# Neighbourhood scores with zero-padded queries, bias and maximum in one instruction, and new planned lengths

## The chip, the cores and the metric

The kernel runs on one core of one Trainium2 chip. The metric is device time in microseconds (us). The figure for the kernel before is the median of three runs. A profile of one further execution supplies every duration below; its span runs from the first to the last instruction of the program, and the execution's own time lies a little above it.

The engines are TensorE (PE in the profile; PEld is its weight loads), VectorE (DVE), ScalarE (ACT), GpSimd (POOL) and SyncE (SP, which here only issues DMAs). TensorE reads SBUF and writes PSUM. Each engine works through its own list of instructions in order and waits on semaphores for the others.

## The reference

Two layers of a diffusion backbone. 256 latent tokens (a grid of 4 rows of 64 columns) and 128 context tokens pass through each layer with the same weights. A layer normalises and modulates its input, projects it once (`w_in`), and splits the columns among three head groups: latent attention (6 heads, "mla"), neighbourhood attention (6 heads of 64, "na"), and differential attention (4 heads, two softmax maps each, "diff"). The outputs are concatenated, projected by `w_out`, added to the residual through a gate, and followed by a gated feed-forward network. The part that the change touches is the neighbourhood attention:

```python
s_win = jnp.einsum('bhrqd,bhrjkd->bhrqjk', qg, kg).astype(jnp.float32) * scale + bias[None].astype(jnp.float32)
s_win = jnp.where(in_win[:, None, :], s_win, NEG)
s_ctx = jnp.einsum('bhrqd,bhcd->bhrqc', qg, k_ctx).astype(jnp.float32) * scale
...
p = jax.nn.softmax(jnp.concatenate([s_win.reshape(b, h, rows, GRID_W, n_win), s_ctx], axis=-1), axis=-1).astype(v.dtype)
```

A latent query thus sees 128 cached context keys without a bias and 256 latent keys with one: the learned bias of the relative position inside a window of 16 columns, and -1e30 outside it. The 128 context queries see the 128 context keys alone. The head size is 64.

## The kernel before

All 384 tokens lie in three tiles of 128 (two latent, `t` = 0 and 1, and one context, `t` = 2). Weights arrive by DMA in `raw` tiles, ACT rounds them to a high part (`wh`, `split_hi`, L254), DVE subtracts to get the low part (`wl`, L260), and each product of the large projections is three matmuls, L321 to L323 (`mm3`).

A layer's front and attention run under a planner. `add` makes a `Task` with an engine, a planned length, the tasks that it follows, the rooms that it takes (`z`, `s` and `t` are PSUM banks; `tok`, `brief`, `e`, `pT`, `pd`, `bias` are SBUF buffers) and a priority. `Plan.order` (L115) simulates all engines with these planned lengths and with `HOPS`, the time from one engine's end to another's start. Whenever an engine is free it takes the ready task of the lowest priority number whose rooms are free. It also models the clock of PE in windows of `WINDOW` = 3.413 us, and doubles PE's planned lengths when a window was little used. The starting times that come out fix the order of the instructions on all five engines; on the chip, an instruction waits in that order, whatever is ready behind it. Planned lengths therefore change no work, only its order.

The dense part of the plan is `g1`, the input projection in six groups of columns (`CHUNKS`): units of six matmuls with the priority `DENSE`, so that they fill PE's time between steps of attention. After them the first three blocks of the output projection (`OUT_EARLY`) play the same part. They write tiles that reuse the space of the dense part's inputs (`o_late`), so most of them can only follow when the dense part is done. Behind the plan, the rest of the output projection and the feed-forward network follow in the order of the program's text, with an order found by the framework's own scheduler.

The path of a neighbourhood head:

- `done_n(j)` takes columns of `g1` for the pair of heads 2j and 2j+1. Per token tile it copies them (L1184), squares (L1199), reduces (L1220), takes the root on POOL (L541, L542), scales (L1223), transposes queries and keys with PE (`turn`, L1209), and writes them to SBUF: `queries` on ACT (L1212) with the gain `naq`, `keys` on DVE (L1215). A pair's two heads lie in rows 0 to 63 and 64 to 127 of the tiles `nu[0]` (queries) and `nu[1]` (keys).
- `near(j)` calls `pair`, which calls `soft` five times: for each of the two heads and the two latent tiles a score of 128 queries against 384 keys, and then both heads' context scores of 128 by 128. `score` (L1037) is one call in float32, which appears as two matmul records, over the 64 rows of its head. `maxima` adds the bias in PSUM (L1100) and finds the maximum (L1045). `exps` (L1056) makes the exponentials and sums on ACT, `norm` the reciprocal (L1061) and the scaling (L1066) on DVE, `turn` transposes the map (L1004), and `evac` copies it out (L1106). When all is there, `out` multiplies by the values (L1139, L1142).
- The bias of a head is a tile of 128 by 6 x 64 floats, loaded from a table that the host builds (`_bias_index`), with two buffers (L1092).
- The latent heads use the same `soft` and `pair` with 96 rows, the differential heads `soft` with 128 rows.

The order of the attention steps is `mla(0)`, `diff(0)`, `mla(1)`, `mla(2)`, and then by `ORDER` `diff(1)`, `diff(2)`, `near(0)`, `diff(3)`, `near(1)`, `near(2)`.

Of the kernel before, what the change touches and what calls it, by code (L numbers as in the profile page):

```python
# [17 lines left out]
P = 128  # L18
# [39 lines left out]
HOPS = {('pe', 'act'): 0.2, ('pe', 'dve'): 0.16, ('act', 'pe'): 0.22, ('dve', 'pe'): 0.27, ('pool', 'dve'): 0.06, ('act', 'dve'): 0.15, ('dve', 'act'): 0.15}  # L58
# [124 lines left out]
def trunk(ctx: ExitStack, tc, xT_d, cv_d, crow_d, pcol_d, prow_d, cache_d, dfk_d, rope_d, bias_d, ident_d,  # L183
# [378 lines left out]
    def parameters(l, staged=None):  # L562
# [14 lines left out]
        naq, lam, nlam, subg = (par.tile([P, 1], F32, tag=t, name=nm(t)) for t in ("naq", "lam", "nlam", "subg"))  # L577
# [35 lines left out]
    for l in range(DEPTH):  # L613
# [177 lines left out]
        def g1(ci, done, kbs=(0, 2, 4, 6), kind="z"):  # L791
# [3 lines left out]
            for kb in kbs:  # L795
# [3 lines left out]
                for t in range(3):  # L799
# [7 lines left out]
                    u = add(PE, 6 * (n / 2400 + 0.003), unit, after=[lo, last[t], hready[kb], hready[kb + 1]],  # L807
# [95 lines left out]
        def up_q(t, pr):  # L903
# [37 lines left out]
            p = add(POOL, 1.6, lambda: rsqrt(x["rs"], x["ms"], 96 * EPS), after=red, prio=pr)  # L941
# [5 lines left out]
        def up_kv(i, pr):  # L947
# [34 lines left out]
            p = add(POOL, 1.6, lambda: rsqrt(x["rs"], x["ms"], mskr[:, i:i + 1]), after=red, prio=pr)  # L982
# [38 lines left out]
        def soft(maps, after, spread, bias=None, joint=None, keep=None):  # L1021
# [18 lines left out]
            def maxima():  # L1040
                if bias:
                    bias(x["b"][0][0])
                x["mx"], i = small(n), 0
                for ps, c in x["b"]:
                    nc.vector.tensor_reduce(x["mx"][:, i:i + c], ps[:, :c, :], axis=AX.X, op=ALU.max, negate=True)  # L1045
                    i += c

            def exps():
                x["su"], x["e"] = small(n), []
                for ps, c in x["b"]:  # L1050
                    for j in range(c):
                        i = len(x["e"])
                        if nk == NT or i == 0:
                            t = e_tile()
                        x["e"].append(t if nk == NT else t[:, i * nk:(i + 1) * nk])
                        nc.scalar.activation(x["e"][i], ps[:, j, :], AF.Exp, bias=x["mx"][:, i:i + 1],  # L1056
                                             accum_out=x["su"][:, i:i + 1])
# [14 lines left out]
            a = add(PE, COST_S * w / NT * (0.25 if joint else 1), score, after=after, take=("s",) * banks, prio=pr + PRS)  # L1072
            b = add(DVE, 0.08 * banks + 1.05e-3 * w + (0.34 if bias else 0), maxima, after=[a], prio=pr + PRM)
# [11 lines left out]
        def pair(kt, qk, v, h0, biased, after, vals, late=None):  # L1085
# [3 lines left out]
            for i in range(2) if biased else ():  # L1089
                def fetch(i=i):  # L1090
                    p["bias", i] = wk.tile([P, 6, 64], F32, tag="bias", name=nm("bias"))
                    nc.sync.dma_start(p["bias", i], bias_d[l, :, h0 + i])  # L1092
                ld[i] = add(DMA, 0.3, fetch, take=("bias",), prio=seq[0])
                in_line("bias", ld[i])
            vs, scored, rooms = [], [], []
            for i in range(2):
                for t in range(2):
                    def bias(ps, i=i, t=t):
                        u0 = 2 - 2 * t
                        nc.vector.tensor_tensor(ps[:, 0, P:NT], ps[:, 0, P:NT],  # L1100
                                                p["bias", i][:, u0:u0 + 4, :].rearrange("p u c -> p (u c)"), op=ALU.add)
# [15 lines left out]
                    else:  # L1117
# [51 lines left out]
        nu, na_ready, na_room = [], [[] for _ in range(3)], []  # L1169
        vn, vn_ready = [], [[] for _ in range(3)]  # L1170

        def na_units():
            nu.extend(units(3, P))
            dma.dma_start(nu[1][:, :, 0:P], cache_d[l, :, CA_NAK:CA_NAK + 384].rearrange("p (a b) -> p a b", a=3))

        def done_n(j):
            hd = slice(2 * j, 2 * j + 2)

            def done(t, z, unit, room):
# [31 lines left out]
                def queries():  # L1211
                    nc.scalar.activation(nu[0][:, j, t * P:(t + 1) * P], x["pt"][:, 0], AF.Copy, scale=naq)  # L1212
# [16 lines left out]
                na_ready[j].append(add(ACT, 0.26, queries, after=[f], frees=[f], prio=pr))  # L1229
# [6 lines left out]
        def done_d(p):  # L1236
            hd = slice(2 * p, 2 * p + 2)

            def done(t, z, unit, room):
# [45 lines left out]
                d = add(POOL, 1.9, lambda: rsqrt(x["rs"], x["ms"], EPS), after=[c], prio=pr)  # L1285
                e = add(DVE, 0.33, lambda: nc.vector.tensor_tensor(heads(x["n"], 8), heads(x["n"], 8), bc3(x["rs"], 32), op=ALU.mult),
                        after=[d], prio=pr)
                df_ready[p][t] = add(DVE, 1.25 if t < 2 else 0.34, rotate, after=[e], frees=[a], prio=pr)
# [4 lines left out]
        def df_unit(h, after, pr):  # L1293
# [19 lines left out]
            for t in range(3):  # L1313
# [29 lines left out]
                d = add(POOL, 0.86, parts_lo, after=[c], prio=pr)  # L1343
                e = add(PE, 0.37, stack, after=[d], take=("t",), frees=[c], prio=pr)
# [7 lines left out]
        def diff_step(h, t, st, after, late=()):  # L1352
# [30 lines left out]
            o = add(PE, 0.6 if t < 2 else 0.16, out, after=[v] + vd_ready[h // 2], take=("t",), frees=[x["room"]], prio=pr + PRO)  # L1383
# [3 lines left out]
        def diff_tail(h, st, late, pr):  # L1387
# [23 lines left out]
            c = add(POOL, 1.0, lambda: rsqrt(st["rs"], st["ms"], EPS), after=[b], prio=pr)  # L1411
# [41 lines left out]
        def near(j):  # L1453
            if not dense:
                dense.extend(t for t in plan.tasks if t.dense)
            sl = [slice(64 * i, 64 * i + 64) for i in range(2)]
            pair(3 + j, lambda: [[u[s, j, :] for s in sl] for u in nu], lambda: vn[min(j, 1)][:, :, slice(0, 2) if j < 2 else slice(2, 4)], 2 * j, True, na_ready[j], vn_ready[j],
                 "row" if j < 2 else "direct")

# [22 lines left out]
        for i, (ms, kb, r) in enumerate(blocks):  # L1482
# [5 lines left out]
            prev = add(PE, 0.93, lambda ms=ms, kb=kb: ms.mm(kb), after=[ld, prev, fin], frees=[ld] if ld else [], prio=DENSE / 2)  # L1488
# [144 lines left out]
def _bias_index():  # L1633

    p = np.arange(P)
# [8 lines left out]
    return np.where(inw[:, None, :], idx, 15 * 31)  # L1644
# [89 lines left out]
```

## Time and profile before

| | |
|---|---|
| median of three runs | 1035.77 us (1035.76 to 1036.49) |
| the profiled execution | 1036.13 us |
| its span | 1034.4 us |
| mean granted TensorE clock | 0.986 |
| PE busy | 1012.3 us, 6074 matmul records |
| DVE, ACT, POOL busy | 719.5, 509.1, 172.7 us |
| DMA | 162.25 MB, mean 157 GB/s |

The span has four kinds of stages. The first hundred us load and project; attention of layer 0 ends near 214 us; the output projection and feed-forward network of layer 0 run to about 530 us; layer 1 has its attention from about 575 to 723 us and its feed-forward network to the end. Busy time of PE is taken from matmul records whose ends are modelled, so the starts of successive records are the better measure of what a piece costs. A clock figure of 1.00 in the windows view means full clock and 0.50 half.

### The profile page before, as it was taken

The page shows a single profiled execution, that of the slowest core. Times are in us where ns is not written, and L with a number is a line of the kernel's source. Part 1 is how long each engine was busy: PE and PEld are TensorE (multiplying, and loading weights), DVE is VectorE, ACT ScalarE, POOL GpSimd, SP SyncE. Part 2 cuts the span into 40 slices and gives each one's busy share as a digit, 9 for nine tenths or more (in the row PEclk, how much of TensorE's full clock was granted, in tenths as well). Part 3 has the DMA queues.
Part 4 walks back from the last instruction along what each step waited for, and adds up shares of the span by engine and source line. Part 5 has one row for each costly group of instructions (what it writes and reads, how often), then busy time and mean ns, then how long its engine had stood idle before and what let it go on. Part 6 is the DMA issues. An engine that isn't in the chain of part 4 may idle for free.

```text
span 1034.4 us, 16528 instructions
## 1 busy us (share of the span) xinstructions
PE 1012.3 (98%) x6074; PEld 933.0 (90%) x6074; DVE 719.5 (70%) x1599; ACT 509.1 (49%) x1180; POOL 172.7 (17%) x263
## 2 busy tenths in 40 slices
PE   8999999989999999999999999989999999999998
PEld 7877779679999999999978878867999999999998
DVE  5677787955999999963455887766869755554332
ACT  3466778745433333343326668766653334333221
POOL 2266223201001001100024533230010000000000
PEclk9999999989999999999999999969999999999999
DMA  9865444125575757684463232410376434343441
GB/s 356 331 202 190 161 153 138 58 82 202 165 243 185 233 177 232 206 273 131 123 226 101 81 125 71 154 54 9 123 249 199 125 120 137 108 123 111 139 137 42
DMA packets 129681, 162.25 MB, mean 157 GB/s; under 512 B 5056, under 2 KB 111680, under 8 KB 127296
## 3 DMA queue, kind: packets, MB, share of 16 engines
q1 hardware_dynamic: 121184, 132.76, 40.3%
q0 software_dynamic: 6832, 27.77, 7.7%
q8 instruction: 48, 0.79, 0.3%
q10 hardware_dynamic: 1584, 0.66, 0.2%
q14 instruction: 33, 0.27, 0.1%
HBM read 158.12 MB, written 3.05 MB: 156 GB/s over the span
## 4 chain that ended last, share of the span: by engine, by line
PE 76%; DVE 2%; ACT 1%; POOL 1%; issue 1%; ACTq 0%; DVEq 0%; POOLq 0%
PE z L321 11%; PE z L323 11%; PE z L322 11%; PE t L322 6%; PE t L321 6%; PE t L323 6%; PE s L322 5%; PE s L323 5%; PE s L321 5%; PE s L1037 2%; PE t L1004 2%; PE t L1139 1%; POOL small L542 1%; PE t L1376 1%; PE z L1037 1%
## 5 line engine op out<-in xcount | busy, mean ns | idle before, releaser
L254 ACT ACTIVATE wh<-raw 128x1024 fp32r<-128x1024 f32 (+2 forms) x216 | 201.5, 934 | 366.0 <-PE z L322 138.8
L260 DVE TENSOR_TENSOR wl<-raw,wh 128x1024 fp32r<-128x1024 f32 (+2 forms) x216 | 230.7, 1070 | 111.6 <-ACT wh L254 111.2
L321 PE MATMUL z<-fh,wh 128*128 128x386 f32 x304 | 103.2, 339 | 0.0
L322 PE MATMUL z<-fl,wh 128*128 128x386 f32 x304 | 103.0, 339 | 0.0
L323 PE MATMUL z<-fh,wl 128*128 128x386 f32 x304 | 102.6, 338 | 0.0
L444 DVE CUSTOM_DVE_ANT_0 sums<-wt,sums,pcol 128x1024 f32<-128x1024 f32 x80 | 102.2, 1278 | 0.3 <-DVE small L1578 0.3
L321 PE MATMUL z<-wh,hh 128*128 128x384 f32 (+1 forms) x264 | 99.9, 379 | 1.1 <-ACT hh L514 0.5
L323 PE MATMUL z<-wh,hl 128*128 128x384 f32 (+1 forms) x264 | 90.3, 342 | 0.5 <-DVE hl L522 0.5
L322 PE MATMUL z<-wl,hh 128*128 128x384 f32 (+1 forms) x264 | 89.8, 340 | 0.0
L542 POOL TENSOR_TENSOR small<-small,mhalf 128x4 f32<-128x4 f32 (+4 forms) x58 | 73.2, 1262 | 4.8
L321 PE MATMUL s<-fh,wh 128*128 128x386 f32 x200 | 68.2, 341 | 0.0
L321 PE MATMUL t<-fh,wh 128*128 128x386 f32 x200 | 68.1, 340 | 0.0
L322 PE MATMUL t<-fl,wh 128*128 128x386 f32 x200 | 67.8, 339 | 0.0
L322 PE MATMUL s<-fl,wh 128*128 128x386 f32 x200 | 67.8, 339 | 0.0
L323 PE MATMUL t<-fh,wl 128*128 128x386 f32 x200 | 67.5, 338 | 0.0
L323 PE MATMUL s<-fh,wl 128*128 128x386 f32 x200 | 67.5, 338 | 0.0
L438 POOL DMA_DIRECT2D wt<-in_w_modT x40 | 21.5, 539 | 273.7 <-DVE mod L444 190.8
L321 PEld LDWEIGHTS z<-wh,hh 128*128 128x128 f32 x264 | 49.8, 189 | 9.2 <-issue 4.2
L322 PEld LDWEIGHTS z<-fl,wh 128*128 128x128 f32 x304 | 57.5, 189 | 0.0
L323 PEld LDWEIGHTS z<-fh,wl 128*128 128x128 f32 x304 | 57.3, 188 | 0.0
L321 PEld LDWEIGHTS z<-fh,wh 128*128 128x128 f32 x304 | 57.2, 188 | 0.0
L1056 ACT ACTIVATE e<-s,small 128x384 f32<-128x384 f32 (+1 forms) x102 | 51.0, 506 | 12.2 <-DVE small L1045 11.2
(316 smaller groups left out, 2422.8 us busy)
## 6 DMA issues: line engine op xcount, KB each, us to landing
raw<-in_w_gate SPq DMA_DIRECT2D x22, 1024.0 KB, 6.0
raw<-in_w_up SPq DMA_DIRECT2D x22, 1024.0 KB, 5.4
raw<-in_w_down SPq DMA_DIRECT2D x32, 704.0 KB, 4.8
wt<-in_w_modT POOLq DMA_DIRECT2D x40, 512.0 KB, 4.3
raw<-in_w_mod SPq DMA_DIRECT2D x16, 1024.0 KB, 5.0
raw<-in_w_in SPq DMA_DIRECT2D x40, 384.0 KB, 3.9
raw<-in_w_out SPq DMA_DIRECT2D x8, 1024.0 KB, 5.5
qu<-in_w_mod SPq DMA_DIRECT2D x8, 512.0 KB, 7.4
```

Of the source, the lines that this page charges most:

```text
L254: nc.scalar.activation(hi, src, AF.Copy)
L260: nc.vector.tensor_tensor(lo, src, hi.bitcast(F32), op=ALU.subtract)
L321: nc.tensor.matmul(out, sh, mh, start=first, stop=False)
L322: nc.tensor.matmul(out, sh, ml, start=False, stop=False)
L323: nc.tensor.matmul(out, sl, mh, start=False, stop=last)
L438: nc.gpsimd.dma_start(self.w[:, self.loaded % 3], w_modT[l, c * P:(c + 1) * P])
L444: nc.vector.tensor_tensor_reduce(self.junk, self.w[:, self.n % 3], self.s[:, v], 1.0, pcol[l][:, PC_BMOD + c:PC_BMOD + c + 1], ALU.mult, A ...
L542: nc.gpsimd.tensor_tensor(out, t[:, :n], mhalf[:, :n], op=ALU.pow)
L1004: nc.tensor.transpose(pt[:, b, :], x, ident)
L1037: nc.tensor.matmul(ps[:, i, :], q, k, start=True, stop=True)
L1056: nc.scalar.activation(x["e"][i], ps[:, j, :], AF.Exp, bias=x["mx"][:, i:i + 1], accum_out=x["su"][:, i:i + 1])
L1139: nc.tensor.matmul(po[64 * i:64 * i + 64, 0:NL], vv[:, b, v0 + i, :], p["pT"][i][:, b, :], start=(b == 0), stop=(b == 2), tile_position=(0 ...
```

## The change

Five edits.

1. **Padded queries.** `queries` now writes each head into a tile of its own, 128 rows high. The gain `naq` becomes two columns, each with zeros in the other head's 64 rows, so that one ACT instruction per head writes its queries and zeros. That is two instructions of 128 by 128 in place of one. Four such tiles exist (the three columns of `nu[0]` and a new tile `qn`); heads take them in turn, so pair 2 reuses those of pair 0. The keys stay as they are, both heads above each other, and a score contracts over all 128 rows.
2. **A new order constraint.** For that reuse, the transposes of pair 2 (`na_last`) follow all scores of `near(0)`, its context scores included.
3. **Context scores in one bank.** Both heads' context scores now go to one PSUM bank, and one reduction finds both maxima.
4. **Bias and maximum in one pass.** `tensor_tensor_reduce` adds the bias to all 384 keys, multiplies by -1, writes back to PSUM and gives the minimum, which is the negated maximum that `exps` needs. The exponential then uses scale -1. The bias tile grows to 128 by 5 x 128 floats, with a block of zeros for the context keys; a query tile takes blocks 0, 2, 4 or 0, 1, 2.
5. **Planned lengths.** `HOPS` and the planned lengths of some dozen tasks change; nothing that they stand for is changed.

```diff
-HOPS = {('pe', 'act'): 0.2, ('pe', 'dve'): 0.16, ('act', 'pe'): 0.22, ('dve', 'pe'): 0.27, ('pool', 'dve'): 0.06, ('act', 'dve'): 0.15, ('dve', 'act'): 0.15}
+HOPS = {('pe', 'act'): 0.22, ('pe', 'dve'): 0.22, ('act', 'pe'): 0.22, ('dve', 'pe'): 0.27, ('pool', 'dve'): 0.18, ('dve', 'pool'): 0.18, ('act', 'dve'): 0.15, ('dve', 'act'): 0.13}
...
+            nc.vector.memset(naq, 0.0)
+            for i in range(2):
+                h = slice(64 * i, 64 * i + 64)
+                nc.vector.tensor_scalar(naq[h, i:i + 1], pc[h, PC_NAQ:PC_NAQ + 1], 0.125, None, op0=ALU.mult)
...
-                    u = add(PE, 6 * (n / 2400 + 0.003), unit, after=[lo, last[t], hready[kb], hready[kb + 1]],
+                    u = add(PE, 6 * (n / 2400 + 0.0135), unit, after=[lo, last[t], hready[kb], hready[kb + 1]],
...
-            p = add(POOL, 1.6, lambda: rsqrt(x["rs"], x["ms"], 96 * EPS), after=red, prio=pr)
+            p = add(POOL, 2.1, lambda: rsqrt(x["rs"], x["ms"], 96 * EPS), after=red, prio=pr)
...
             def maxima():
+                x["mx"], i = small(n), 0
                 if bias:
-                    bias(x["b"][0][0])
-                x["mx"], i = small(n), 0
+                    s = x["b"][0][0][:, 0, :]
+                    s = s.rearrange("p (b k) -> p b k", k=P)
+                    nc.vector.tensor_tensor_reduce(s, s, bias(), -1.0, 3e38, ALU.add, ALU.min, x["mx"])
+                    return
...
-                                             accum_out=x["su"][:, i:i + 1])
+                                             scale=-1.0 if bias else 1.0, accum_out=x["su"][:, i:i + 1])
...
-            a = add(PE, COST_S * w / NT * (0.25 if joint else 1), score, after=after, take=("s",) * banks, prio=pr + PRS)
-            b = add(DVE, 0.08 * banks + 1.05e-3 * w + (0.34 if bias else 0), maxima, after=[a], prio=pr + PRM)
+            a = add(PE, (0.22 if joint else COST_S) * w / NT, score, after=after, take=("s",) * banks, prio=pr + PRS)
+            b = add(DVE, 0.08 * banks + 1.05e-3 * w + (0.06 if bias else 0), maxima, after=[a], prio=pr + PRM)
...
-                    p["bias", i] = wk.tile([P, 6, 64], F32, tag="bias", name=nm("bias"))
+                    p["bias", i] = wk.tile([P, 5, P], F32, tag="bias", name=nm("bias"))
...
-            x, a, e, pr = soft(lambda: [(qk()[0][i][:, NL:NT], qk()[1][i][:, NT:512], i == 0 or biased) for i in range(2)], after,
-                               (P, 2, 2 if biased else 1), keep="pd")
+            x, a, e, pr = soft(lambda: [(qk()[0][i][:, NL:NT], qk()[1][i][:, NT:512], i == 0) for i in range(2)], after,
+                               (P, 2, 1), keep="pd")
...
+            qn = ws.tile([P, NT], F32, name=nm("qn"))
+            nu[0] = [nu[0][:, i, :] for i in range(3)] + [qn]
...
-                    nc.scalar.activation(nu[0][:, j, t * P:(t + 1) * P], x["pt"][:, 0], AF.Copy, scale=naq)
+                    for i in range(2):
+                        nc.scalar.activation(nu[0][(2 * j + i) % 4][:, t * P:(t + 1) * P], x["pt"][:, 0], AF.Copy, scale=naq[:, i:i + 1])
...
+                if j == 2:
+                    na_last.append(f)
-                na_ready[j].append(add(ACT, 0.26, queries, after=[f], frees=[f], prio=pr))
+                na_ready[j].append(add(ACT, 0.53, queries, after=[f], frees=[f], prio=pr))
...
-            pair(3 + j, lambda: [[u[s, j, :] for s in sl] for u in nu], ...
+            scored, _ = pair(3 + j, lambda: [[nu[0][(2 * j + i) % 4] for i in range(2)], [nu[1][:, j, :]] * 2], ...
+            for t in na_last if j == 0 else ():
+                for a in scored:
+                    a.then.append(t)
+                    t.need += 1
```

Further planned lengths, old to new: the roots on POOL 1.6 to 2.1, 1.9 to 2.2 and 1.0 to 1.18; the rotation of differential heads 1.25 to 1.35 and 0.34 to 0.42; their low parts on POOL 0.86 to 0.98; their stacking on PE 0.37 to 0.47; their product with the values 0.6 to 0.67 and 0.16 to 0.23; a block of modulation matmuls 0.93 to 1.0.

More of the change, by code (lines that the diff above doesn't have):

```diff
@@ L1090, in fetch @@
                 def fetch(i=i):
-                    p["bias", i] = wk.tile([P, 6, 64], F32, tag="bias", name=nm("bias"))
+                    p["bias", i] = wk.tile([P, 5, P], F32, tag="bias", name=nm("bias"))
                     nc.sync.dma_start(p["bias", i], bias_d[l, :, h0 + i])
-                ld[i] = add(DMA, 0.3, fetch, take=("bias",), prio=seq[0])
+                ld[i] = add(DMA, 0.6, fetch, take=("bias",), prio=seq[0])
                 in_line("bias", ld[i])
@@ L1166, in mla_pair @@
             return pair(j, lambda: [[mlu[h // 3][w][:, h % 3, :] for h in hs] for w in range(2)], lambda: vm, 2 * j, False, after, vals)
-        nu, na_ready, na_room = [], [[] for _ in range(3)], []
+        nu, na_ready, na_room, na_last = [], [[] for _ in range(3)], [], []
         vn, vn_ready = [], [[] for _ in range(3)]
@@ L1342, in df_unit @@
                 c = add(ACT, 0.56, parts_hi, after=[a, df_ready[h // 2][t]], take=("tok",), prio=pr)
-                d = add(POOL, 0.86, parts_lo, after=[c], prio=pr)
-                e = add(PE, 0.37, stack, after=[d], take=("t",), frees=[c], prio=pr)
+                d = add(POOL, 0.98, parts_lo, after=[c], prio=pr)
+                e = add(PE, 0.47, stack, after=[d], take=("t",), frees=[c], prio=pr)
                 out.append(add(ACT, 0.27, queries, after=[e], frees=[e], prio=pr))
@@ L1382, in diff_step @@
             v = add(ACT, 0.38 if t < 2 else 0.2, evac, after=[e], frees=[e], prio=pr + PRT)
-            o = add(PE, 0.6 if t < 2 else 0.16, out, after=[v] + vd_ready[h // 2], take=("t",), frees=[x["room"]], prio=pr + PRO)
+            o = add(PE, 0.67 if t < 2 else 0.23, out, after=[v] + vd_ready[h // 2], take=("t",), frees=[x["room"]], prio=pr + PRO)
             st["kept"] = st.get("kept", []) + [add(ACT, 0.2, keep, after=[o], frees=[o], prio=pr + PRO)]
@@ L1410, in diff_tail @@
                     after=[a], frees=[a], prio=pr)
[L1411 removed]
+            c = add(POOL, 1.18, lambda: rsqrt(st["rs"], st["ms"], EPS), after=[b], prio=pr)
             d = add(DVE, 0.28, scaled, after=[c] + ([st["mate"]] if h % 2 else []), take=() if h % 2 else ("row",), prio=pr)
@@ L1643, in _bias_index @@
     idx = dr[:, :, None] * 31 + rc[:, None, :]
-    return np.where(inw[:, None, :], idx, 15 * 31)
+    idx = np.where(inw[:, None, :], idx, 15 * 31)
+    out = np.full((P, 5, P), 15 * 31 + 1)
+    for b, u in ((1, 0), (2, 2), (4, 4)):
+        out[:, b] = idx[:, u:u + 2].reshape(P, P)
+    return out
 def _rope_table():
```

23 lines of the change are left out of this document (10 added, 13 removed).

## Prediction

> **What bounds the kernel now.** I read the page's busy times and slices first, then the busy times by stage, then the timeline of PE.
>
> ```profile
> span 1034.4 us, 16528 instructions
> PE 1012.3 (98%) x6074; PEld 933.0 (90%) x6074; DVE 719.5 (70%) x1599; ACT 509.1 (49%) x1180; POOL 172.7 (17%) x263
> ...
> PE 76%; DVE 2%; ACT 1%; POOL 1%; issue 1%; ACTq 0%; DVEq 0%; POOLq 0%
> ```
>
> PE is busy for 98% of the span and holds 76% of the chain of waits; no other engine holds more than 2%. The windows view gives the stages (PE, PEld, DVE, ACT, POOL busy with instruction counts, then clock, DMA share, GB/s):
>
> ```profile
> 130.00:180.00 50.00, 50.00 (x353) 42.37 (x352) 39.72 (x105) 41.08 (x140) 15.59 (x30) 1.00 0.47 146
> 180.00:220.00 40.00, 37.77 (x232) 28.07 (x230) 29.77 (x90) 27.59 (x83) 6.78 (x10) 1.00 0.13 41
> 580.00:660.00 80.00, 77.25 (x471) 63.88 (x470) 65.42 (x174) 57.89 (x178) 35.34 (x49) 1.00 0.32 98
> 660.00:700.00 40.00, 37.38 (x183) 29.17 (x182) 27.32 (x71) 26.28 (x86) 10.40 (x18) 0.74 0.32 101
> ```
>
> In attention PE is busy for 202.4 of these 210 us; DVE and ACT lie between 66% and 82% of a stage. A microsecond taken from PE there is nearly a microsecond of time, as long as dense units are left to put in its place. But 660 to 700 has a mean clock of only 0.74. In finer windows:
>
> ```profile
> 671.50:674.90 3.40, 3.40 (x24) 3.36 (x23) 3.22 (x8) 3.40 (x15) 0.84 (x2) 1.00 0.23 69
> 674.90:678.30 3.40, 2.27 (x15) 1.66 (x14) 2.52 (x7) 2.98 (x12) 2.93 (x5) 1.00 0.76 259
> 678.30:681.70 3.40, 3.08 (x9) 1.71 (x9) 3.17 (x11) 2.28 (x11) 2.79 (x5) 0.50 0.03 5
> 681.70:685.10 3.40, 3.40 (x11) 1.99 (x11) 2.98 (x8) 1.74 (x3) 1.26 (x3) 0.50 0.07 19
> 685.10:688.50 3.40, 2.45 (x11) 1.73 (x9) 2.08 (x5) 2.72 (x11) 0.87 (x2) 0.50 0.20 58
> 688.50:692.00 3.50, 3.27 (x15) 3.15 (x15) 1.72 (x7) 2.13 (x10) 0.00 (x0) 0.50 0.00 0
> 692.00:695.40 3.40, 3.40 (x7) 1.41 (x7) 2.31 (x8) 1.61 (x5) 0.00 (x0) 0.50 0.00 0
> 695.40:698.80 3.40, 3.40 (x14) 1.93 (x15) 1.37 (x5) 1.66 (x5) 0.92 (x2) 0.50 0.00 0
> ```
>
> One window with PE busy for 2.27 of 3.40 us, in which ACT was busy for 2.98, is followed by six at half clock, 20.5 us. PE looks full in several of them and the clock still does not come back; from 692.00, seven long matmuls fill a whole window. These 20.5 us hold the scores of `near`'s second pair of heads.
>
> **1. Padded queries: PE.** The timeline of PE gives start, duration, line and count; differences of starts are the cost. First a 64-row score (0.84 = 199.35 - 198.51) between transposes, then the same with 96 rows:
>
> ```profile
> 197.61 0.49 PE L1037 MATMUL s<-ku,qu 64*128 64x128 f32 x4
> 198.03 0.55 PE L1004 MATMUL t<-ident,e 128*128 128x128 f32 x3
> 198.51 0.91 PE L1037 MATMUL z<-ku,qu 64*128 64x384 f32 x2
> 199.35 0.44 PE L1004 MATMUL t<-ident,e 128*128 128x128 f32 x2
> ...
> 606.44 0.81 PE L1037 MATMUL s<-ku,qu 96*128 96x384 f32 x2
> 607.09 0.49 PE L1004 MATMUL t<-ident,e 128*128 128x128 f32 x3
> 607.42 0.84 PE L1037 MATMUL s<-ku,qu 96*128 96x384 f32 x2
> ```
>
> The 96-row score takes 607.09 - 606.44 = 0.65 us, the 64-row one 0.84: 0.19 more for the same 384 columns. Three transposes between two 64-row groups take 198.51 - 198.03 = 0.48, between 96-row groups 0.33: 0.15 more for one way out and one way in. I read both as one effect: rows "64*128" are another division of the array than "96*128" and "128*128", and at each change PE finishes what it has, and does not load weights ahead. A padded score has 128 rows. Its price lies between that of 64 rows (no gain, rival D) and that of 96 rows, which it resembles in having no other division; I take the latter.
>
> ```profile
> L1037 PE MATMUL s<-ku,qu 64*128 64x384 f32 x34 | 15.8, 574 | 0.1
> ...
> L1037 PE MATMUL z<-ku,qu 64*128 64x384 f32 x14 | 7.6, 639 | 0.0
> ...
> 187.66 1.55 PE L1037 MATMUL z<-ku,qu 64*128 64x384 f32 x4
> ...
> 712.12 0.91 PE L1037 MATMUL s<-ku,qu 64*128 64x384 f32 x2
> ```
>
> 48 records are 24 scores. Counted along PE's timeline they stand in 20 visits, 8 in layer 0 and 12 in layer 1: one score like the last row, which is the last visit, or two in a row like the row above it, with 1.55 us instead of 2 x 0.65 = 1.30. Each visit saves 0.19 to 0.25 inside and 0.15 around it, 0.34 taken: 20 x 0.34 = **6.8 us**. The six context visits (0.42 = 198.03 - 197.61, both heads) become full-height too; the 96-row form of the same takes
>
> ```profile
> 108.15 0.61 PE L1037 MATMUL s<-ku,qu 96*128 96x128 f32 x4
> 108.59 0.27 PE L1004 MATMUL t<-ident,e 128*128 128x128 f32 x1
> ```
>
> 0.44, so they lose 0.02 and save 0.15: 6 x 0.13 = **0.8 us**. Together 7.6 us of PE. The dense units give PE other work in most of attention, but not behind 675; a tenth is taken off for what then becomes waiting: **-6.9 us**.
>
> A rule speaks against padding: the Trainium skill, "TensorEngine Tiling (Array Packing)", section When to Use Tiling, would split the array for a contraction of 64 rows and run two such products at once. By it the six context pairs would double, 6 x 0.42 = 2.5 us, and the sum would be 4.4 instead of 6.9. The trace doesn't bear it out: two heads' context scores take 0.42 against 0.44 for two 96-row ones, and the large scores do not overlap.
>
> **2. Queries: ACT.**
>
> ```profile
> L1212 ACT ACTIVATE qu<-t,naq x17: 359/367/388, 130.1 to 682.2; 128x128 f32<-128x128 f32 x17
> ```
>
> 18 more instructions at 0.367 us: 6.6 us of ACT. Where PE has dense units this is hidden, ACT having 9 of 50 us free between 130 and 180. Not hidden is what falls on 671 to 678, where ACT had 6.38 of 6.80 us: three of them, 1.1 us. Taken: **+1 us** (0 to +3.3, one layer's nine).
>
> **3. Bias and maximum: DVE.**
>
> ```profile
> L444 DVE CUSTOM_DVE_ANT_0 sums<-wt,sums,pcol 128x1024 f32<-128x1024 f32 x80 | 102.2, 1278 | 0.3 <-DVE small L1578 0.3
> ...
> L1100 DVE TENSOR_TENSOR s<-s,bias 128x256 f32<-128x256 f32 x17 | 7.2, 426 | 1.4 <-PE s L1037 1.2
> ...
> L1045 DVE TENSOR_REDUCE small<-s 128x1 f32<-128x384 f32 x67 | 35.7, 552 | 4.6 <-PE s L1037 3.7
> ```
>
> Removed: 0.426 + 0.552 = 0.978 us per score. Added: the same operation over 384 in PSUM, not in this trace; the 1024-wide one in SBUF takes 1.278. The bounds are 0.552 (a plain pass over 384) and 1.278 (no cheaper than 1024 wide); an estimate with the slope between the two passes over 256 and 384, (552 - 426)/128 = 0.98 ns an element, gives 1.278 - 640 x 0.00098 = 0.65, nearest to the lower end. So 24 x 0.33 = 8 us of DVE go. That is work beside PE, which is the bound; taken at **0**. Were DVE waited for at every score, it would be 24 x -0.43 = -10 at one bound and 24 x 0.30 = +7 at the other.
>
> **4. Context in one bank, larger bias, new constraint.** One reduction over both heads' maxima removes about nothing. It needs one `s` bank, so context scores can be planned sooner. The bias load grows from 192 to 320 KB:
>
> ```profile
> bias<-in_bias SPq DMA_DIRECT2D x12, 192.0 KB, 3.1
> ...
> raw<-in_w_in SPq DMA_DIRECT2D x40, 384.0 KB, 3.9
> ```
>
> Between 3.1 and 3.9 us to landing. The planner puts it a buffer ahead, and DMA has a share of 0.13 in 180 to 220; 0 (to +0.8 for a late one of the last pair, where scores of `near(2)` wait in DVE's list and everything behind them there). The constraint puts the transposes of pair 2 behind `near(0)`'s context scores. In layer 1 they stand side by side already:
>
> ```profile
> 676.73 0.41 PE L1209 MATMUL t<-ident,tok 128*128 128x128 f32 x2 [0.28 <-ACT e L1056]
> ...
> 677.07 0.76 PE L1037 MATMUL s<-ku,qu 64*128 64x128 f32 x4
> ```
>
> So the new wait is 677.07 + 0.76 - 676.73 = 1.1 us at most in that order, and 0 if one bank lets the context scores come sooner, which I take. Behind the waiting transposes on PE stand the context scores themselves; three `tok` buffers stay held meanwhile, for which `diff(3)` would wait.
>
> **5. Planned lengths.** A dense unit is planned 0.978 long before and 1.041 after. The row
>
> ```profile
> 606.09 0.34 PE L322 MATMUL z<-wl,hh 128*128 128x384 f32 x1
> ```
>
> and the score at 606.44, with one matmul more between them, put one at 0.175 and the unit of six at 1.05.
>
> The new plan is truer there. What that can win is PE's idle time in these four stages, 7.6 us, and the half-clock windows; what it can lose has no row. I take 0 by itself, -5 to +6.
>
> **6. The half clock of layer 1.** It began when one window lacked PE work: the plan had let its dense units run out, and ACT had 2.98 us of 3.40. It lasted because drained 64-row scores and short matmuls leave the array partly idle. The change acts on both: more even planning, and scores without drains in just these windows. At full clock, the 19.0 us that PE is busy in the six rows would halve, but DVE's 13.6 us do not: 20.5 - 13.6 = 6.9 at most. I take **-6 us**, 0 if the dip stays. The Trainium skill, "TensorE: Matmul & The Clock Gate", section "What's actually happening", says that about 3.4 us of busy PE restore full clock; here two rows with PE busy 3.40 of 3.40 did not, so "busy" in this view is not what the clock goes by.
>
> **Sum.** 1036.13 (profiled execution, 0.36 above the median of 1035.77; 1.7 above its span) - 6.9 + 1 - 6 = **1024.2 us**. I say 1024.
>
> **Rivals.**
>
> *A: the dip stays.* The same gap in PE's work between dense units and output units comes back, as ACT has three instructions more there. For it: six rows without recovery at full "busy". 1036.1 - 6.9 + 1 = 1030.
>
> *B: the second hole closes too.*
>
> ```profile
> 217.50:220.90 3.40, 2.15 (x9) 0.94 (x7) 2.02 (x7) 3.40 (x7) 0.00 (x0) 1.00 0.00 0
> 220.90:224.30 3.40, 0.98 (x3) 0.98 (x4) 3.35 (x5) 2.04 (x6) 0.00 (x0) 0.50 0.00 0
> 224.30:227.70 3.40, 3.40 (x13) 3.40 (x12) 2.63 (x6) 0.00 (x0) 0.00 (x0) 0.50 0.93 292
> ```
>
> Behind the plan of layer 0, PE idles 1.25 + 2.42 us and then runs 6.8 us at half clock. A plan that ends with more output work left would cover it; nothing in the change aims there. 3.7 idle + 1.7 (half of the last row): 1024 - 5 = 1019; with less idle time in attention 1017.
>
> *C: slower.* In layer 0's last stage (180 to 220) the same mixture of work ran at full clock, with 2.23 us idle. PE now has less to do per step, while ACT has more; dense units run out sooner. Once a window of 3.4 us there falls to the 2.27 us of the row at 674.90, layer 0 gets its own half-clock stretch: as long as layer 1's, 6.9 us by the reckoning of step 6, up to 10 (half of 20.5), plus as much idle time again as now (2.2). With the old dip kept: 1030 + 6.9 to 10 + 2.2 = 1039 to 1042, say 1040. It decides at that one window's work.
>
> *D: padding does nothing.* If the excess belongs to float32 scores of this place and not to 64 rows, or if waits eat it, the time stays at 1036. Against it: the same instruction with 96 rows, and the same neighbours, does not have it.
>
> **How the numbers follow.** Forecast (1024) 0.45; A (1030) 0.25; B (1017) 0.13; D (1036) 0.07; C (1040) 0.10. The range leaves out D and C and the fast end of B: 1014 to 1034; the unknown sizes of steps 2, 3 and 5 lie inside it. Forecast, A and B are all faster by more than 0.2% (2.1 us, about what a measurement of this kernel can tell from no change): 0.83 less 0.01 for a weak A: 0.82. D and the mild end of C: same 0.08. The rest of C: slower 0.10.
>
> **What would show it.** Step 1: L1037 has no 64-row form left, a padded score takes 0.65 us from its start to the next piece, three transposes between scores 0.33, and PE's busy time falls. Step 2: L1212 has 36 instructions. Step 3: one instruction of about 0.65 us at `maxima` for near. Step 6: the granted clock is 1.00 in the windows of layer 1's late attention; six at 0.50 again are A; new ones at 0.50 before 215 us are C. The forecast is wrong if PE's busy time falls by 7 us and the span doesn't: then PE waits where it did not, and the window's ACT and DVE rows say for whom.

## The result and the profile after

| | before | after |
|---|---|---|
| median of four runs each | 1036.13 us (1035.76 to 1037.82) | 1024.90 us (1021.03 to 1028.36) |
| ratio, 95% interval | | 0.9888, 0.985 to 0.9925 |
| profiled execution, its span | 1036.13, 1034.4 us | 1021.03, 1019.2 us |
| mean granted clock | 0.986 | 0.998; in the three other runs 0.993, 0.989, 0.992 |

A second measurement of the changed kernel gave 1023.96 us (1023.29 to 1024.59), ratio 0.9878 (0.9866 to 0.9891). The profiled execution above is the fastest of its four runs, so its trace shows 15.2 us of span gone where the medians show 11 to 12.

The page of the changed kernel, busy times and chain of waits:

```profile
span 1019.2 us, 16546 instructions
...
PE 995.8 (98%) x6074; PEld 928.2 (91%) x6074; DVE 710.5 (70%) x1597; ACT 509.7 (50%) x1198; POOL 170.3 (17%) x263
...
PE 86%; DVE 4%; ACT 4%; POOL 2%; issue 1%; DMA 1%; SPq 0%; ACTq 0%; DVEq 0%; POOLq 0%
```

PE is still the bound. Its busy time fell by 16.5 us; the gaps between its records, summed over the trace, rose from 17.1 to 18.5 us. So the gain is PE work that takes less time, not fewer waits.

The windows view of the changed kernel by stages (PE, PEld, DVE, ACT and POOL busy, then clock, DMA share, GB/s), with the three windows behind layer 0's plan among them:

```profile
130.00:180.00 50.00, 47.66 (x339) 37.35 (x339) 38.80 (x115) 40.50 (x140) 11.50 (x22) 1.00 0.47 147
180.00:220.00 40.00, 36.02 (x239) 31.60 (x238) 29.50 (x86) 30.98 (x103) 10.82 (x19) 1.00 0.10 31
217.50:220.90 3.40, 3.40 (x22) 3.40 (x21) 3.40 (x6) 3.40 (x9) 0.00 (x0) 1.00 0.13 21
220.90:224.30 3.40, 3.40 (x21) 3.40 (x20) 3.40 (x9) 2.00 (x5) 0.00 (x0) 1.00 0.84 287
224.30:227.70 3.40, 3.40 (x21) 3.40 (x20) 3.40 (x9) 2.27 (x4) 0.00 (x0) 1.00 0.73 225
580.00:660.00 80.00, 79.18 (x501) 68.17 (x499) 64.85 (x173) 62.81 (x198) 29.03 (x43) 1.00 0.38 124
660.00:700.00 40.00, 34.79 (x214) 27.60 (x214) 30.87 (x90) 31.69 (x109) 10.15 (x18) 0.96 0.25 76
```

Two stretches of half clock are gone or shorter. Behind layer 0's plan PE is full at clock 1.00 in all three windows, where it had idled and then run at half clock. And the stage from 660 to 700 has a clock of 0.96 in place of 0.74. The trace of the second measurement (`after_again`) shows both as well. What the change gave back is in the first two rows: between 130 and 220 PE is now idle for 6.3 of 90 us, before for 2.2. There the second measurement even has a new stretch at half clock, 6.8 us from 196.8, which the faster execution above lacks.

The clock's own record has one stretch at half left in this stage, 690.8 to 694.3. Windows laid along it:

```profile
687.40:690.80 3.40, 1.72 (x8) 0.90 (x7) 3.29 (x11) 2.55 (x8) 0.00 (x0) 1.00 0.00 0
690.80:694.20 3.40, 3.40 (x13) 2.62 (x15) 2.67 (x11) 2.39 (x11) 0.00 (x0) 0.51 0.00 0
```

A window with 1.72 us of PE work still costs the clock, but now for a single window of 3.4 us and not for six.

The padded scores, in PE's timeline of the changed kernel (start, duration, line, count):

```profile
202.74 0.49 PE L1009 MATMUL z<-ident,e 128*128 128x128 f32 x3
203.06 0.81 PE L1042 MATMUL s<-ku,qu 128*128 128x384 f32 x2
203.71 1.00 PE L1388 MATMUL t<-vd,pd 128*128 128x64 f32 x8
```

203.71 - 203.06 = 0.65 us for a score and 203.06 - 202.74 = 0.32 for three transposes ahead of it: as a 96-row score, and against 0.84 and 0.48 with 64 rows. The pass for bias and maximum, by shape:

```profile
L1051 DVE DVE_READ_ACCUMULATOR2_ANT small<- x24: 83/142/144, 149.4 to 699.5; 128x1 f32 x24
L1051 DVE CUSTOM_DVE_ANT_0 s<-s,bias x10: 555/567/597, 151.8 to 694.4; 128x384 f32<-128x384 f32 x10
L1051 DVE CUSTOM_DVE_ANT_1 s<-s,bias x8: 550/560/567, 148.9 to 697.5; 128x384 f32<-128x384 f32 x8
```

It is 0.56 us, and 0.14 more to read the result out: 0.70 where 0.65 was estimated and 0.978 stood before. These are sums of durations. Neighbours overlap a little: two passes in a row occupy 0.99 us (starts from 156.47 to 157.46 in DVE's timeline).

### The profile page after: what moved, and what is told of

Read it like the earlier page. It is cut to its first block, busy times and chain, and to the rows that moved or that the text cites. A ratio compares the mean times of both kernels' runs of the same rounds, so it can differ in the third digit from the quotient of the medians.

```text
span 1019.2 us, 16546 instructions
## 1 busy us (share of the span) xinstructions
PE 995.8 (98%) x6074; PEld 928.2 (91%) x6074; DVE 710.5 (70%) x1597; ACT 509.7 (50%) x1198; POOL 170.3 (17%) x263
## 4 chain that ended last, share of the span: by engine, by line
PE 86%; DVE 4%; ACT 4%; POOL 2%; issue 1%; DMA 1%; SPq 0%; ACTq 0%; DVEq 0%; POOLq 0%
PE z L321 13%; PE z L322 12%; PE z L323 12%; PE t L322 6%; PE t L321 6%; PE t L323 6%; PE s L321 6%; PE s L322 6%; PE s L323 6%; PE s L1042 3%; PE t L1009 2%; PE m L372 2%; PE t L1145 1%; PE s L916 1%; POOL small L542 1%
## 5 line engine op out<-in xcount | busy, mean ns | idle before, releaser
L1065 ACT ACTIVATE e<-s,small 128x384 f32<-128x384 f32 (+1 forms) x106 | 53.4, 512 | 11.1 <-DVE small L1054 9.9
## 6 DMA issues: line engine op xcount, KB each, us to landing
raw<-in_w_gate SPq DMA_DIRECT2D x22, 1024.0 KB, 5.8
raw<-in_w_up SPq DMA_DIRECT2D x22, 1024.0 KB, 5.4
raw<-in_w_mod SPq DMA_DIRECT2D x16, 1024.0 KB, 5.4
raw<-in_w_out SPq DMA_DIRECT2D x8, 1024.0 KB, 5.6
```

## The experiments

Each ran in rounds beside the kernel before. The median of that kernel moved by up to 1.4 us between groups of runs, so the gain here is (1 - ratio) x 1036 us. Span, PE busy, PE idle (the gaps between its records) and the time at half clock (from the clock's record, without the stretch that runs past the end of the span) are of the one profiled execution.

| kernel | median us | ratio (95%) | gain us | span | PE busy | PE idle | half clock |
|---|---|---|---|---|---|---|---|
| before | 1036.1 | 1 | 0 | 1034.4 | 1012.3 | 17.1 | 27.3 |
| after | 1024.9 | 0.9888 (0.985, 0.9925) | 11.6 | 1019.2 | 995.8 | 18.5 | 3.4 |
| after_again | 1024.0 | 0.9878 (0.9866, 0.9891) | 12.6 | 1021.5 | 1000.5 | 16.1 | 13.7 |
| e1_rows64 | 1037.0 | 0.9992 (0.9981, 1.0004) | 0.8 | 1033.7 | 1014.6 | 14.1 | 30.7 |
| e2_pad_only | 1031.4 | 0.9931 (0.9917, 0.9946) | 7.1 | 1026.4 | 1002.1 | 19.4 | 10.2 |
| e3_lengths_only | 1026.2 | 0.9889 (0.987, 0.9907) | 11.5 | 1024.4 | 1005.7 | 13.7 | 13.7 |
| e4_old_lengths | 1031.6 | 0.9939 (0.9923, 0.9955) | 6.3 | 1030.2 | 1005.9 | 19.3 | 17.1 |
| e5_two_passes | 1033.4 | 0.9972 (0.9959, 0.9984) | 2.9 | 1034.2 | 1006.3 | 23.0 | 23.9 |
| e6_lengths_pad | 1022.4 | 0.9864 (0.9849, 0.9878) | 14.1 | 1021.4 | 999.2 | 17.2 | 6.8 |
| e7_fine_constraint | 1024.0 | 0.9893 (0.9874, 0.9912) | 11.1 | 1022.5 | 1001.1 | 16.4 | 13.7 |
| e8_one_pass | 1021.9 | 0.9856 (0.9842, 0.9869) | 14.9 | 1020.3 | 998.9 | 16.4 | 6.8 |
| e9_truer | 1026.7 | 0.9897 (0.9881, 0.9914) | 10.7 | 1021.9 | 1000.2 | 16.8 | 6.8 |
| e10_nudge | 1023.9 | 0.9854 (0.983, 0.9878) | 15.1 | 1023.4 | 1002.8 | 15.6 | 17.1 |
| e11_two_passes_planned | 1033.3 | 0.9963 (0.995, 0.9976) | 3.8 | 1031.4 | 1006.8 | 19.6 | 20.5 |

The theory after the result: the padding gives the drains and most of layer 1's dip, and the lengths only decide whether the hole behind layer 0's plan closes. The rival: the lengths do nearly all of it.

### The padding in the order of after

The kernel after, with only the large scores back on 64 rows; PE and ACT keep the same order of instructions.

```diff
-[(qk()[0][i][:, t * P:(t + 1) * P], qk()[1][i][:, 0:NT], True)]
+[(qk()[0][i][64 * i:64 * i + 64, t * P:(t + 1) * P], qk()[1][i][64 * i:64 * i + 64, 0:NT], True)] if biased else ...
```

> The changed kernel with its 24 large neighbourhood scores back on the 64 rows of their head; everything else stays, the order of every engine's instructions too. Theory (each visit to another division of the array costs 0.34 us of PE): 20 to 24 visits, +6.8 to +8.2 us of PE's time, 1031 to 1034 us, and the stretches at half clock are no shorter. Rival (the gain is the new plan's, and padding is worth little): within 2 us of the changed kernel, 1023 to 1027. Second rival (waits, not drains, eat PE's time where the scores stand): +2 to +4.

Nothing of the change's gain is left: 1037.0 us, 11 to 12 us above the change by the ratios, and above the ranges of theory and rivals alike. The drains of its 22 visits, at 0.34, are 7.5 of that. The windows view shows the rest:

```profile
150.15:153.60 3.45, 2.40 (x17) 1.51 (x13) 2.63 (x8) 3.18 (x13) 1.10 (x2) 0.99 0.03 7
153.60:157.00 3.40, 3.40 (x12) 1.99 (x10) 2.45 (x10) 1.83 (x7) 2.54 (x6) 0.50 0.41 116
157.00:160.40 3.40, 3.40 (x11) 2.21 (x10) 2.08 (x7) 1.58 (x7) 0.87 (x2) 0.50 0.00 1
```

and in PE's timeline of the same kernel, inside them:

```profile
154.17 1.65 PE L1042 MATMUL s<-ku,qu 64*128 64x384 f32 x2
155.75 0.69 PE L1218 MATMUL t<-ident,tok 128*128 128x128 f32 x2
```

After a thin window the clock stays at half for three windows in which PE looks full, with a 64-row score taking 155.75 - 154.17 = 1.58 us in each of the first two. With padded scores the same order ran at 1.00 there in after and `after_again`. This isn't one unlucky execution: e1's twelve runs have mean clocks of 0.980 to 0.988, the four of after_again 0.993 or 0.994. At half clock PE loses at most half the time, so 0.985 against 0.993 is at most 0.008 x 1034 = 8 us beside the 7.5.

### The padding in the order of before

The kernel before with padded queries (five query tiles in place of four, so that no new constraint is needed); PE's order is that of before.

```diff
-nc.scalar.activation(nu[0][:, j, t * P:(t + 1) * P], x["pt"][:, 0], AF.Copy, scale=naq)
+for i in range(2):
+    nc.scalar.activation(nu[0][(2 * j + i) % 5][:, t * P:(t + 1) * P], x["pt"][:, 0], AF.Copy, scale=naq[:, i:i + 1])
```

> The kernel before with padded queries alone (two ACT instructions for the queries, five query tiles, no new constraint), with the old planned lengths, bias pass and context banks, so that the order is that of before. Theory: 7.6 us of PE go and ACT gives back up to 1; if the stretch of layer 1 at half clock lasted because of drains it shrinks from 20.5 us to 3 to 10 as well, 1022 to 1027; if it lasted because of the order, 1029 to 1031. Rival (the new lengths made the gain): 1034 to 1037.

7.1 us gained, with the drains and the dip together: layer 1's half clock falls from 20.5 to 3.4 us (678.7 to 682.1), and the hole stays. Its windows:

```profile
217.50:220.90 3.40, 2.04 (x8) 0.89 (x6) 2.02 (x6) 3.40 (x7) 0.00 (x0) 1.00 0.00 0
220.90:224.30 3.40, 1.09 (x3) 1.09 (x4) 3.35 (x6) 1.92 (x6) 0.00 (x0) 0.56 0.03 2
224.30:227.70 3.40, 3.40 (x12) 3.40 (x12) 2.51 (x5) 0.00 (x0) 0.00 (x0) 0.50 0.98 298
660.00:700.00 40.00, 36.84 (x229) 32.28 (x227) 32.95 (x86) 32.78 (x110) 10.57 (x18) 0.96 0.32 99
```

PE's busy time falls by 10.2 us, its idle time rises by 2.3. So full-height scores do bring the clock back, as step 6 had it: the one half-clock window left, with PE busy for 3.3 of 3.4 us, is followed by full clock. But drains and dip together give about 7 us in this order, not the 12.9 written down (11.9 with step 2's loss).

### The planned lengths alone

The kernel before with the change's hops and planned lengths, and nothing else (64-row scores, two passes). The lengths of the pieces that the change itself alters (queries, pass of bias and maximum, load of the bias) stay as they were.

```diff
-HOPS = {('pe', 'act'): 0.2, ('pe', 'dve'): 0.16, ...
+HOPS = {('pe', 'act'): 0.22, ('pe', 'dve'): 0.22, ...
-u = add(PE, 6 * (n / 2400 + 0.003), unit, ...
+u = add(PE, 6 * (n / 2400 + 0.0135), unit, ...
...
```

> The kernel before with the new planned lengths alone (hops, roots, rotations, dense units, stacking, products of differential attention), no other edit. Theory: the drains stay, so PE's busy time stays near 1012; what moves is the half-clock stretch and the hole behind layer 0's plan, 1030 to 1038. Rival (the plan made the gain): 1022 to 1028 with no half-clock stretch.

11.5 us, as much as the whole change. Its windows:

```profile
217.50:220.90 3.40, 3.40 (x22) 3.40 (x21) 1.91 (x5) 2.09 (x3) 0.00 (x0) 1.00 0.00 0
220.90:224.30 3.40, 3.40 (x20) 3.28 (x20) 3.40 (x7) 3.08 (x7) 0.00 (x0) 1.00 0.41 123
224.30:227.70 3.40, 3.40 (x21) 3.40 (x21) 3.40 (x9) 2.83 (x6) 0.00 (x0) 1.00 0.60 198
660.00:700.00 40.00, 35.54 (x193) 26.76 (x193) 29.71 (x82) 28.46 (x101) 9.97 (x17) 0.87 0.27 84
```

The hole is closed and layer 1's half clock is 10.2 us instead of 20.5. No instruction was removed, yet PE's busy time is 6.6 us lower (the clock) and its idle time 3.4: the 10.0 us of span. The rival holds for the total. Nor did the lengths only close the hole: most of the 10 us came in layer 1, as the split by layer below shows. Lengths and padding attack the same half-clock time there, so their gains do not add.

The converse, after with the old lengths (again without those of the altered pieces), is e4:

> The changed kernel with the old planned lengths put back (those of the neighbourhood pieces that the change itself alters stay). Theory: drains are gone here too, 1024 to 1031. Rival (the lengths made the gain): 1034 to 1038.

6.3 us are left of about 12. In the new structure too, the lengths are worth some 6.

### Lengths and padding together, without the rest

e3 and e2 together: PE's order is that of e3, the passes stay two (426 and 552 ns), the context scores keep two banks, and there is no new constraint.

> The kernel before with the new planned lengths and padded queries, in the order of the run with the lengths alone; the bias keeps its two passes, the context scores their two banks, and five query tiles make the new constraint needless. Theory (padding is worth 0.34 us a visit in any order, and the order is a cast of its own): 1026.2 less 6 to 8, 1018 to 1020, faster than the whole change. Rival (padding and lengths cure the same loss, the half clock, and do not add): 1024 to 1027.

14.1 us, no less than the whole change; the time lies between the theory's range and the rival's. In e3's order the padding adds 2.6 us, with intervals that overlap; in before's it gave 7 and in after's 11 to 12. The work removed is much the same in each; what differs most is half-clock time: 13.7 to 6.8 us, 27.3 to 10.2, and 30.7 to 3.4 or 13.7.

The traces can also be split by layer. The matmuls of `norm_sum` stand at the start of a layer and at the start of its feed-forward part. In all 14 traces the two stretches from a feed-forward norm on take the same time, 273.9 and 276.5 to 276.6 us. Apart from the 12 to 13 us ahead of the first norm, every difference therefore lies in the two stretches between a layer's first norm and its feed-forward norm (us, one execution each):

| | before | e2, padding | e3, lengths | e6, both | after | after_again |
|---|---|---|---|---|---|---|
| layer 0 | 241.3 | 241.5 | 238.1 | 235.9 | 236.6 | 239.0 |
| layer 1 | 230.0 | 221.9 | 223.4 | 222.2 | 219.6 | 219.8 |

In layer 1, where the long dip was, padding alone takes off 8.1 us, the lengths alone 6.6 and both together 7.8: the same loss, cured twice. In layer 0 the padding alone takes off nothing (PE's busy time there falls by 1.1 us and its idle time rises by 1.3), the lengths, which close the hole, 3.2, and both together 5.4.

### Bias and maximum in two passes

After with an addition and a maximum, both over all 384 keys, in place of the one pass, at the same places in every list.

```diff
-nc.vector.tensor_tensor_reduce(s, s, bias(), -1.0, 3e38, ALU.add, ALU.min, x["mx"])
+nc.vector.tensor_tensor(s, s, bias(), op=ALU.add)
+nc.vector.tensor_reduce(x["mx"], x["b"][0][0][:, 0, :], axis=AX.X, op=ALU.max, negate=True)
```

> The changed kernel with bias and maximum as two DVE instructions again (an addition over 384 and a maximum over 384), planned lengths and so the planned order untouched. The one pass was measured at 0.57 + 0.14 us, the two passes should take 0.55 + 0.55: 0.4 us more of DVE for each of 24 scores. Theory (DVE lies beside PE): 0 to +2 us against the changed kernel. Rival (DVE stands on the chain from score to transpose where the dense units have run out): +4 to +8.

9.7 us slower than after_again, more than the theory (0 to 2) and the rival (4 to 8) allowed. DVE has 24 x (1.12 - 0.70) = 10 us more (11.4 by the busy times of the two pages, 722.2 and 710.8), and was busy for 70% of the span; by step 3's reckoning this time should have been hidden. DVE's timeline of e5 shows where it isn't:

```profile
156.55 0.55 DVE L1051 TENSOR_TENSOR s<-s,bias 128x384 f32<-128x384 f32 x1
157.14 0.56 DVE L1052 TENSOR_REDUCE small<-s 128x1 f32<-128x384 f32 x1
157.61 0.56 DVE L1051 TENSOR_TENSOR s<-s,bias 128x384 f32<-128x384 f32 x1
158.20 0.56 DVE L1052 TENSOR_REDUCE small<-s 128x1 f32<-128x384 f32 x1
158.68 0.74 DVE L1354 CAST ku<-t 128x256 fp32r<-128x256 f32 x2
```

PE's timeline of e5 at the same place:

```profile
156.35 1.11 PE L1348 MATMUL t<-identr,tok 128*128 128x128 f32 x8 [0.45 <-DVE ku L1226]
159.14 2.83 PE L1146 MATMUL t<-pT,vm 128*64 128x256 f32 x12 [1.68 <-DVE ku L1354]
```

and that of after:

```profile
156.27 1.11 PE L1347 MATMUL t<-identr,tok 128*128 128x128 f32 x8 [0.28 <-DVE ku L1225]
157.93 1.52 PE L1145 MATMUL t<-pT,vm 128*64 128x256 f32 x12 [0.55 <-DVE ku L1353]
```

Two scores' passes stand in DVE's list ahead of the copies of keys that PE's next work needs. They end 1.1 us later, and PE waits 1.68 us instead of 0.55. The windows of e5:

```profile
154.77:158.18 3.41, 2.24 (x14) 1.48 (x13) 3.29 (x10) 2.25 (x8) 1.92 (x5) 1.00 0.09 29
158.18:161.60 3.42, 2.46 (x12) 1.49 (x14) 2.29 (x7) 1.17 (x5) 0.00 (x0) 0.50 0.32 96
161.60:165.00 3.40, 3.40 (x16) 2.61 (x13) 0.98 (x3) 1.38 (x5) 0.00 (x0) 0.50 0.20 58
```

and of after:

```profile
154.77:158.18 3.41, 2.59 (x18) 1.78 (x18) 3.34 (x14) 2.39 (x9) 1.84 (x5) 1.00 0.09 28
158.18:161.60 3.42, 3.42 (x30) 2.47 (x27) 2.00 (x8) 2.33 (x8) 0.00 (x0) 1.00 0.52 148
161.60:165.00 3.40, 3.40 (x22) 2.72 (x21) 2.82 (x11) 3.04 (x11) 0.00 (x0) 1.00 0.02 6
```

PE's work in the first window falls from 2.59 to 2.24 us, the next two windows run at half clock, and the 12 products that take 1.52 us in after take 2.83. The transposes behind all this start at 165.24 us in e5 and at 161.23 in after: a wait longer by 1.1 us has cost about 4 here. The rest of the 9.7 us was not followed place by place; the clock's record of e5 has one more stretch at half than after_again's in layer 1 as well (680.4 and 704.3 against 691.7).

Two runs ask whether this depends on the order. e8 is e6 with the one pass in place of its two (planned length as before, two context banks, four query tiles); PE's order is that of e6:

> The run with lengths and padding, with the bias and the maximum as one pass, the larger bias tile and four query tiles added, and the planned length of the two passes kept, so that PE's order is the same. Against that run's ratio of 0.9864 to the kernel before. Theory from the two-pass run (+9.4 us in the changed kernel's order: DVE is on the chain where dense units have run out): 24 scores get 0.28 us shorter, and half of them are waited for: -2 to -5 us, ratio 0.982 to 0.985. Rival (the loss there came from a plan that did not know of the second pass): 0 to -1, ratio 0.9855 to 0.9865.

0.8 us gained, for 24 x (0.978 - 0.70) = 6.7 us of DVE. The busy times of e6 and then of e8, from their pages:

```profile
PE 999.2 (98%) x6074; PEld 929.8 (91%) x6074; DVE 717.6 (70%) x1603; ACT 508.9 (50%) x1198; POOL 167.9 (16%) x263
```

```profile
PE 998.9 (98%) x6074; PEld 929.2 (91%) x6074; DVE 709.8 (70%) x1603; ACT 508.7 (50%) x1198; POOL 168.2 (16%) x263
```

7.8 us of DVE are gone and PE does not notice, so the rival's number came, though the next run refutes its reason. e11 is e5 with the two passes' true length in the plan:

```diff
-b = add(DVE, 0.08 * banks + 1.05e-3 * w + (0.06 if bias else 0), maxima, after=[a], prio=pr + PRM)
+b = add(DVE, 0.08 * banks + 1.05e-3 * w + (0.62 if bias else 0), maxima, after=[a], prio=pr + PRM)
```

> The changed kernel with two passes for bias and maximum, as in the run that lost 9 us, but with their planned length at the 1.11 us that they take there (2 x 0.56) instead of 0.54. Theory (the loss came from an order made for a pass that is shorter than the real one): most of it returns, 1024 to 1028, ratio 0.988 to 0.992. Rival (DVE's own time is on the chain of scores whatever the order): 1031 to 1035, ratio 0.995 to 0.998.

1033.3 us: the loss stays. That e5 lost because the plan did not know of its longer passes is refuted. The stage from 670 to 700 in the windows view of e11 and then of after:

```profile
670.00:700.00 30.00, 25.60 (x127) 19.54 (x129) 23.80 (x63) 22.75 (x78) 8.44 (x15) 0.83 0.20 62
```

```profile
670.00:700.00 30.00, 26.55 (x162) 19.75 (x161) 24.12 (x76) 24.13 (x81) 6.33 (x10) 0.94 0.21 63
```

With the length known, layer 0 is nearly as fast as in after_again (the next layer's first norm starts at 526.0 us against 525.2; e5 has 530.9), and layer 1 is not: here PE is busy for 0.95 us less than in after, at a clock of 0.83 instead of 0.94. Why these passes cost 9 us here and the old ones under 1 in e6's order, where the difference in DVE work is 6.7 us against 10, I can't say beyond that place.

### The constraint, and truer lengths

e7 lets each of pair 2's transposes wait only for the scores of its own token tile. e9 gives the plan the measured 0.73 for two queries and 0.70 for the pass with its bias. e10 moves two planned lengths of after by 0.01 us (2.2 to 2.19, 1.0 to 0.99), as a measure of what an arbitrary reshuffling does. after_again is the kernel after once more.

> The changed kernel, with the transposes of the last pair's tile t held only by the first pair's scores of the same tile, not by all of them. Theory (the constraint costs at most 1.1 us): within 3 us of the changed kernel either way, by the new order alone. Rival (the constraint makes the waits of late attention): 1019 or less, and PE's idle time between 580 and 700 us falls by 3 or more.

> The changed kernel with two more planned lengths set to what its own profile shows: 0.73 for the two query instructions (planned 0.53, measured 2 x 0.37) and 0.70 for the pass of bias and maximum (planned 0.54, measured 0.57 + 0.14). Theory (a truer plan wastes less): 1018 to 1022. Rival (every new order is a draw, and truth of a length does not show): 1022 to 1032.

> The changed kernel with two planned lengths moved by 0.01 us (2.2 to 2.19 for a root on POOL, 1.0 to 0.99 for a block of modulation matmuls), which says nothing about the chip. It measures how much the order alone moves the time. Theory (the order is a draw): it differs from the changed kernel's 1024 by 2 to 8 us either way. Rival (orders close to each other take the same time): within 1.5 us.

> The changed kernel once more, as the common measure on this chip: 1021 to 1028, differing from run to run by how many windows of PE run at half clock.

e7's lists for PE and ACT came out the same as after's, so loosening the constraint frees nothing; e7 is in effect a third measurement of after. e9's plan is truer and no faster (0.9897 against 0.9878, intervals overlapping). In e10 the trace has another kind of record than after's at 657 of 6074 places of PE's list, and the time is the same within the intervals (0.9854 against 0.9878).

No version clearly beats the change: e10 (0.9854), e8 (0.9856) and e6 (0.9864) have intervals that overlap after_again's (0.9866 to 0.9891), at most about 2.5 us better.

## Why the prediction was right, and which steps were not

The time, 1024 us, was right, as was the sign. By its parts the sum was right only because errors cancelled, which is luck: for steps 1, 2 and 6 it had 11.9 us where e2 gained 7.1, and for step 5 it had 0 where the lengths brought 7.0 on top (e6 against e2). The rest of the change, at 0 in the sum, gained nothing clear of the intervals: after lies 1.5 to 2.5 us behind e6.

- **Step 1, padding (-6.9).** The mechanism holds: 0.65 us a score, 0.32 for three transposes, no form of 64 rows left. Its worth is not one number: 2.6, 7 and 11 to 12 us in three orders, clock included. e1 and e2 refute rival D, that padding does nothing. But the 3.1 us written down for layer 0 (8 x 0.34 + 3 x 0.13) came to nothing in before's order: PE waited instead.
- **Step 6, half clock (-6).** Layer 1's dip shrank from six windows to one, by full-height scores as expected (e2). In layer 1 steps 1 and 6 had 4.5 us of drains and 6 of clock, and e2 gained 8.1 there with 17 us less at half clock; drains and clock can't be told apart in it, so the size of 6 is not tested by itself. The step also named more even planning as a cause, and that holds: the lengths alone halved the dip (e3). Rival A did not come.
- **Step 5, lengths (0): the step that failed.** The prediction said that a truer plan could win PE's idle time and the half-clock windows, and then took nothing for it. Alone it gave 11.5 us, beyond the step's own range of 5. In e3's trace 3.2 us of this came in layer 0, where the lengths closed the hole behind the plan; that is the mechanism of rival B, and "nothing in the change aims there" was wrong. The larger part, 6.6 us, came in layer 1, most of it from the half-clock windows that the step had named and priced at nothing.
- **Step 3, one pass (0).** 0.70 us against the estimate of 0.65. "Work beside PE" holds in e6's order (0.8 us) and fails in after's (9.7 for a pair of passes that is longer than the old one). The step's bound of 10 assumed DVE waited for at every score; what e5's trace shows, at the one place followed, is a wait of 1.1 us more that costs a stretch of half clock.
- **Step 2, queries (+1).** 36 instructions:

```profile
L1222 ACT ACTIVATE qu<-t,naq x28: 348/367/424, 133.7 to 681.6; 128x128 f32<-128x128 f32 x28
...
  PE t L1009: 1.3, 3
```

with the 8 others in rows of the same size. The second row is one of those that list who waited for them: PE's transposes, 1.3 us in three waits. No run took these instructions away by themselves, so the +1 is consistent, not tested.
- **Step 4 (0).** Loosening the constraint gains nothing (e7); the changed order without any constraint was not run. The larger bias lands in 3.5 us, inside the 3.1 to 3.9 of the estimate; the single context bank wasn't tried alone.

```profile
bias<-in_bias SPq DMA_DIRECT2D x12, 320.0 KB, 3.5
```

- **Rival C (slower).** Its price did not come, but its sign did, in part: new half clock before 215 us. The trace of `after_again` has 6.8 us of it from 196.8, and e7's, with the same lists, from 198.0; in layer 0 after_again is 2.4 us slower than the execution without it. e1 (153.6 and 204.8, 10.2 and 6.8 us) and e5 (158.2) show the mechanism too.

## What to carry to other kernels

Where a planner fixes the order of all engines, measure its new lengths alone: they can be worth as much as the work removed. Compare a part of a change in one fixed order, and expect its worth to differ in another, since gains that shorten the same half-clock stretches do not add. Before "hidden beside the bound engine" is set to zero, look for the places where the bound engine's next work stands behind that instruction in its list, and for the clock in the windows after them.

## What the runs showed of the hardware

- **The granted clock differs from run to run of one program, and the time with it.** Five runs of e10: clock 1.000 took 1018.99 us, 0.998 1020.14, 0.993 1023.90, 0.992 1025.67 and 0.991 1025.15. So about 0.9% of clock is 6 us here. The Trainium skill, "TensorE: Matmul & The Clock Gate", section "What's actually happening", says that the gate judges activity in a free-running window of 3413 ns that does not start with the kernel. The clock's record agrees: its stretches at half clock last 3.4, 6.8, 10.2 or 20.5 us, multiples of that window. How a thin place falls into these windows differs between two executions with the same lists. First after_again, whose clock falls at 196.8, then after, whose clock stays:

```profile
193.40:196.80 3.40, 1.57 (x10) 1.02 (x8) 3.36 (x11) 3.37 (x10) 0.00 (x0) 0.99 0.00 0
196.80:200.20 3.40, 2.38 (x7) 1.04 (x5) 3.26 (x12) 2.69 (x11) 1.12 (x2) 0.50 0.57 168
```

```profile
192.50:195.90 3.40, 1.86 (x11) 1.37 (x9) 3.00 (x11) 3.37 (x13) 0.00 (x0) 1.00 0.07 19
195.90:199.30 3.40, 1.79 (x10) 1.24 (x11) 3.33 (x9) 2.69 (x8) 1.12 (x2) 1.00 0.22 57
```

That this makes the whole spread between runs is only argued. Nor is PE's busy time alone what decides: 1.79 us of 3.4 kept the clock here, while windows with 2.6 us lost it in nine other traces, between 521 and 536 us.
- **A window that looks full can keep the clock at half** where it holds 64-row scores. The 14 traces have 62 whole windows of 3.4 us at half clock ahead of the last 5 us of the span. Eight of them have PE busy from end to end with 1.5 to 2.7 us of 64-row scores among its work; each is followed by another window at half. In 42 PE is busy for 3.17 us or more with at most 0.61 us of such scores; each is followed by full clock. The other 12, eleven of them with PE busy for at most 3.1 us and one for 3.21, are followed by half clock. Whether the drains of these scores do it or their using only 64 rows can't be told apart here.
- **Reading out the accumulator takes 142 ns** behind each of the 24 passes, about a fifth of the summed durations.
